# State-space stage: corrections by halves, written orders at the outputs, other slots for gating weights, two conditioning tiles held

## The chip, the cores and the metric

The kernel runs on one core of a Trainium2 chip. The metric is the device time of one execution in microseconds; smaller is better. The core's engines are TensorE (PE: matrix products, with its weight loads as PEld), VectorE (DVE), ScalarE (ACT), GpSimd (POOL) and SyncE (SP), which here only issues DMAs. Each engine has a queue of its own, and engines wait for each other by semaphores.

## What is computed

Four residual layers over 256 tokens of width 1024, all in float32, in sequence: a state-space layer with a gated feed-forward network (FFN), latent attention with an FFN, a layer with a delta-rule memory, and one with differential attention. The change touches the first of them, the state-space stage:

```
shift1, scale1, gate1, shift2, scale2, gate2 = split(silu(c) @ ada_w[0] + ada_b[0], 6)   # conditioning
h = rms_norm(x) * (1 + scale1) + shift1
s[t] = A * s[t-1] + B @ h[t]          # per group of 16 channels a complex diagonal state of 64; 64 groups
y = Re(C @ s) + D * h ;  g = gelu(y)
x = x + gate1 * (g * sigmoid(g @ w_glu + b_glu))       # gating projection
x = x + gate2 * swiglu(rms_norm(x) * (1 + scale2) + shift2)   # first FFN
```

## The kernel before

**Recurrence.** The 256 tokens are 32 chunks of 8. Inside a chunk, the output is a product of the inputs `U` with a Toeplitz kernel (`KM`, four tiles, built by `latest` and `kernels`: transposes, a split into a high and a low part, shifted products, copies by ScalarE). Between chunks the state is carried in `St` (partition = two halves of 64 states, then 32 chunks x real/imaginary x 32 groups). `into` and `turnG` bring each chunk's input into `GT`, transposed. Then VectorE takes seven serial steps, `k` = 1 to 7, over four runs of 8 chunks at once (two products and two sums a step), and then corrects the runs: for `b` = 1 to 3 the state at the end of the run before, times powers `QP`, is added to the seven chunks of run `b` (products into `w1`, sums into `St`). Four accumulators in PSUM (`psY`) hold the outputs, one for each of four blocks. They begin with the products of `U` and `KM`, and `outputs(i)` (line 1006) adds 64 products of `St` with `CE` to block `i` and copies it to `ys`. `gelu(q2)` (1021) transposes two blocks, applies gelu, and splits the result into a high part `gh` (ScalarE) and a low part `gl` (VectorE).

**Weights.** SyncE loads weights as tiles of 1 MB (`wtile`, 356) into a ring of slots: three slots of a pool that lives throughout, and after `deepen(3)` three more, in memory where tiles of the recurrence (pool `old`: `GT`, `w1` among them) lay before. The loads keep their order in the program. A gating tile holds 16 blocks of 128 x 128. `wsplit` cuts it into four pieces, each split into `whi` (ScalarE casts) and `wlo` (VectorE subtracts), and every 128 x 128 block then takes three products (`mm3`, 388). The `whi` pieces lie in slots of tag A (used by `Bm` and `St`), the `wlo` pieces in slots of tag CE (used by `CE`). `proj` (429) runs the gating projection over 64 blocks (192 products).

**Conditioning.** The vectors of the first layer come from 24 tiles of 1 MB (8 of `adaH`, 16 of `ada0`), each multiplied with the replicated activation `crep` in eight products into `ps_gv` (`gemv_rows` 581, `gemv` 595). They are generators: each call of `pump` takes one tile further, that is, issues its load and its products, and with every eighth the result is turned into a column (a ScalarE copy, four transposes, a VectorE sum). Twenty-two pumps stand ahead of the outputs; the two others stand in the gating projection, behind blocks 24 and 48 (`every` = 24).

**Order.** A planner orders the instructions of each engine by estimated times, keeping what `issue_after` and `keep_in_program_order` demand. In stretches under `manual_schedule` the named engines keep the order of the program among the instructions of that stretch; others can still be put between them. Before, TensorE and VectorE have it up to the last `turnG`, and TensorE alone in the outputs:

```
for i in range(3):
    outputs(i)
gelu(0)
outputs(3)
gelu(1)
```

## Time and profile before

| | |
|---|---|
| median of 3 runs (lowest to highest) | 1073.07 us (1072.68 to 1077.14) |
| the profiled execution, its span | 1071.87 us, 1070.1 us |
| busy: PE, PEld, DVE, ACT, POOL | 92%, 82%, 76%, 54%, 25% of the span |
| mean granted TensorE clock | 0.980 |
| read from HBM | 195.3 MB, 184 GB/s over the span |

A row of a timeline has the start (us from the span's start), the busy time, engine, line, operation, and "written<-read" by the program's names with shapes and the count of instructions merged; in square brackets the idle time of the engine before it and what ended that. Matrix products overlap, so busy times of neighbouring rows do too. `ps_gv<-raw,crep` are conditioning products, `ps_mm<-CE,St` output products, `ps_mm<-gh,whi` and the like gating products, `ps_aux<-c_cst,...` transposes. [...]

### The profile page before, as it was taken

What the parts mean: (1) busy time and instruction counts of PE and PEld (TensorE: products, weight loads), DVE (VectorE), ACT (ScalarE), POOL (GpSimd) and SP (SyncE); (2) the same over time, 40 slices, a digit from 0 to 9 for tenths busy, and PEclk for the clock granted to TensorE, in tenths of its full rate; (3) what the DMA queues carried; (4) which work ended last, traced back from release to release, by engine and by line L of the source; (5) the groups of instructions that cost most, each with busy time, mean ns of one, the idle gap of its engine ahead of it and who ended that gap; (6) DMA issues with size and microseconds to landing.
All of it is one profiled execution on the core that took longest, in us unless ns stands there. A gap on an engine that the chain in (4) does not pass through costs nothing.

```text
span 1070.1 us, 21962 instructions
## 1 busy us (share of the span) xinstructions
PE 979.8 (92%) x8474; PEld 873.8 (82%) x8474; DVE 809.3 (76%) x1771; ACT 581.7 (54%) x1304; POOL 266.4 (25%) x302
## 2 busy tenths in 40 slices
PE   3997989999999888989999999988898899899996
PEld 1655978999999866879999999987887786699974
DVE  8774799899995888769665554788887735676995
ACT  6542654555544767746555544565444344575664
POOL 6980100020012650000000011452324133243430
PEclk9999989999999999999999999999999999999998
DMA  9788549887884351256755553331312142265321
GB/s 354 286 329 332 198 158 390 337 308 299 341 335 172 119 177 40 80 197 237 264 174 193 197 176 140 130 128 52 117 41 86 55 158 76 94 231 187 125 80 39
DMA packets 29416, 198.81 MB, mean 186 GB/s; under 512 B 3744, under 2 KB 3872, under 8 KB 6528
## 3 DMA queue, kind: packets, MB, share of 16 engines
q1 hardware_dynamic: 27936, 191.73, 48.2%
q10 hardware_dynamic: 720, 3.15, 0.8%
q0 software_dynamic: 656, 2.53, 0.7%
q8 instruction: 66, 1.08, 0.4%
q14 instruction: 38, 0.31, 0.1%
HBM read 195.30 MB, written 2.10 MB: 184 GB/s over the span
## 4 chain that ended last, share of the span: by engine, by line
PE 71%; DVE 17%; ACT 4%; issue 4%; DMA 2%; POOL 2%; DVEq 0%; POOLq 0%; ACTq 0%; SPq 0%
PE ps_mm L331 52%; PE ps_aux L331 7%; PE ps_aux L334 3%; DVE wlo L310 3%; PE ps_sv L331 3%; PE ps_el L331 2%; DMA raw<-in_ada 2%; PE ps_st L331 2%; PE ps_gv L331 1%; ACT whi L380 1%; DVE Upr L310 1%; DVE D L1796 1%; POOL sq L310 1%; DVE ps_mm L310 1%; DVE shf L323 1%
## 5 line engine op out<-in xcount | busy, mean ns | idle before, releaser
L380 ACT CAST whi<-raw 128x512 fp32r<-128x512 f32 (+2 forms) x488 | 296.2, 613 | 271.3 <-PE ps_mm L331 226.0
L310 DVE TENSOR_TENSOR wlo<-raw,whi 128x512 fp32r<-128x512 f32 (+2 forms) x412 | 288.6, 714 | 127.2 <-ACT whi L380 126.6
L331 PE MATMUL ps_mm<-hh,whi 128*128 128x256 f32 x1064 | 306.8, 290 | 3.9 <-ACT hh L302 2.3
L331 PE MATMUL ps_mm<-hh,wlo 128*128 128x256 f32 x1064 | 300.5, 285 | 1.7 <-DVE wlo L310 1.7
L331 PE MATMUL ps_mm<-hl,whi 128*128 128x256 f32 x1064 | 300.3, 283 | 0.2
L331 PEld LDWEIGHTS ps_mm<-hh,whi 128*128 128x128 f32 x1064 | 202.0, 190 | 9.3 <-ACT hh L302 2.9
L331 PEld LDWEIGHTS ps_mm<-hh,wlo 128*128 128x128 f32 x1064 | 201.2, 190 | 5.9 <-DVE wlo L310 4.1
L331 PEld LDWEIGHTS ps_mm<-hl,whi 128*128 128x128 f32 x1064 | 201.9, 190 | 1.3 <-DVE hl L327 0.6
L310 POOL TENSOR_TENSOR wlo<-raw,whi 128x512 fp32r<-128x512 f32 (+2 forms) x76 | 100.1, 1317 | 241.7 <-ACT whi L380 215.9
L310 POOL TENSOR_TENSOR sq<-sq 128x256 f32<-128x256 f32 x20 | 20.4, 1018 | 406.0 <-ACT sq L302 257.6
L331 PE MATMUL ps_mm<-ah,whi 128*128 128x256 f32 x352 | 99.0, 282 | 0.0
L331 PE MATMUL ps_mm<-al,whi 128*128 128x256 f32 x352 | 98.7, 281 | 0.0
L331 PE MATMUL ps_mm<-ah,wlo 128*128 128x256 f32 x352 | 98.6, 282 | 0.0
L327 DVE SCALAR_TENSOR_TENSOR acc<-raw,cs,acc 128x512 f32<-128x512 f32 x112 | 80.0, 758 | 2.4 <-DMA raw<-in_kvada 1.3
L331 PEld LDWEIGHTS ps_mm<-ah,whi 128*128 128x128 f32 x352 | 67.2, 191 | 0.9 <-ACT whi L380 0.8
L331 PEld LDWEIGHTS ps_mm<-ah,wlo 128*128 128x128 f32 x352 | 66.3, 189 | 1.7 <-DVE wlo L310 0.8
L331 PEld LDWEIGHTS ps_mm<-al,whi 128*128 128x128 f32 x352 | 66.4, 189 | 0.0
L331 PE MATMUL ps_gv<-raw,crep 128*32 128x512 f32 x192 | 29.6, 676 | 19.1 <-DVE ps_mm L310 13.7
L331 PEld LDWEIGHTS ps_gv<-raw,crep 128*32 128x32 f32 x192 | 5.0, 114 | 24.8 <-DVE ps_mm L310 13.7
L331 PE MATMUL ps_mm<-whi,ch 128*128 128x512 f32 x48 | 19.5, 437 | 1.2 <-ACT ch L426 1.2
L331 PE MATMUL ps_mm<-oh,whi 128*128 128x256 f32 x64 | 20.1, 314 | 0.0
L331 PE MATMUL ps_mm<-whi,cl 128*128 128x512 f32 x48 | 19.8, 413 | 0.0
(558 smaller groups left out, 2030.0 us busy)
## 6 DMA issues: line engine op xcount, KB each, us to landing
raw<-in_gu SPq DMA_DIRECT2D x44, 1024.0 KB, 6.7
raw<-in_ada SPq DMA_DIRECT2D x32, 1024.0 KB, 6.2
raw<-in_dn SPq DMA_DIRECT2D x22, 1024.0 KB, 5.4
raw<-in_win SPq DMA_DIRECT2D x15, 1024.0 KB, 5.0
raw<-in_adaH SPq DMA_DIRECT2D x8, 1024.0 KB, 7.3
raw<-in_kvada SPq DMA_DIRECT2D x8, 1024.0 KB, 6.5
raw<-in_ada1h SPq DMA_DIRECT2D x8, 1024.0 KB, 5.8
raw<-in_wout SPq DMA_DIRECT2D x8, 1024.0 KB, 5.0
```

What stands on the lines that cost most here:

```text
L310: return (eng or self.nc.vector).tensor_tensor(out=out, in0=a, in1=b, op=op)
L323: (eng or self.nc.vector).tensor_scalar(out=out, in0=a, scalar1=s1, scalar2=s2, op0=op0, **kw)
L327: return self.nc.vector.scalar_tensor_tensor(out=out, in0=a, scalar=s, in1=b, op0=op0, op1=op1, **kw)
L331: return self.nc.tensor.matmul(out, l, r, start=start, stop=stop, **kw)
L334: return self.nc.tensor.transpose(out, in_, self.ident)
L380: i = self.nc.scalar.copy(out=hi[:, :width], in_=raw[:, o:o + width])
L1796: V.tensor_reduce(out=D_[64 * h:64 * h + 64, 4 * i:4 * i + 4], in_=dm[:, :, h].rearrange("p c b i -> p c i b"), axis=AX.X, op=ALU.add)
```

## The change

- Serial steps: VectorE gets a written order; the low parts of the kernel tiles (`rest`) and their products (`kernels`) stand behind steps 2, 5 and 7. A pump stands behind each step from 2 to 7, one behind the corrections' chain. The input steps pump four times, not twice; the nine pumps between kernel products are gone.
- Corrections: the chain through the run ends comes first; the products and sums then go by halves of the groups (16 of 32), in real and imaginary parts. For this the group axis of `GT`, `St` and `QP` is reordered, so that blocks 0 and 1 read the first 16 places and blocks 2 and 3 the others. `turnG` copies in four pieces, not two. The clearing of `St[:, 0]` moves to GpSimd.
- Outputs: TensorE, ScalarE and VectorE get a written order, with the splits of the first gating tile in it.
- Slots: the ring is counted from 0 at the outputs, so that the next three loads go to the three old slots. The x load stands behind the first gating load. The first `wlo` piece takes a slot of tag C (`Kmat`), the others stay with CE.
- The products of the last two conditioning tiles are held behind `self.gate`: the last gelu transpose, later the last product before their pump. The projection's work on ScalarE and VectorE is held behind the last split of `gelu(1)`.

```diff
@@ gemv
                 for g in range(n):
-                    self.mm(ps[32 * g:32 * g + 32, :], self.crep[:, k, :], ...)
+                    with self.tc.issue_after(self.gate.ins) if self.gate is not None else ExitStack():
+                        self.mm(ps[32 * g:32 * g + 32, :], self.crep[:, k, :], ...)
@@ turnG
-                    S_.copy(out=GT[:, :, ri, 8 * j2:8 * j2 + 8].rearrange("p c (j q) -> p j q c", j=2), in_=...)
+                    for jl in range(2):
+                        j = 2 * j2 + jl
+                        o = GT[:, :, ri].rearrange("p c (a j b) -> p a j b c", a=2, j=8)[:, :, j]
+                        S_.copy(out=o, in_=g[:, jl])
@@ input steps
-                if n in (1, 3):
+                if n < 4:
                     self.pump()
@@ serial steps and corrections
-            V.memset(St[:, 0], 0.0)
+            G.memset(St[:, 0], 0.0)
+            with tc.manual_schedule(engines={mybir.EngineType.DVE}):
+                rest = latest(1)
                 for k in range(1, 8):
...
+                    if k in (2, 5, 7):
+                        q = (2, 5, 7).index(k) + 1
+                        rest()
+                        kernels(q, [])
+                    if k in (3, 5):
+                        rest = latest(2 if k == 3 else 3)
+                    if k > 1:
+                        self.pump()
+                for b in range(1, 3):
...
+                self.pump()
+                runs = St.rearrange("p (b k) r g -> p b k r g", k=8)[:, 1:4]
+                for h in range(2):
+                    f = slice(16 * h, 16 * h + 16)
+                    for r in range(2):
+                        o = runs[:, :, 1:8, r, f]
+                        ws = []
+                        for e in range(2):
+                            w1 = B8("P", [128, 3, 7, 16], "w1", 4)
+                            ws.append(w1)
+                            q = QP[:, (0, 1 + r)[e], 0:7, f].unsqueeze(1).to_broadcast([128, 3, 7, 16])
+                            self.mul(w1, runs[:, :, 0:1, r ^ e, f].to_broadcast([128, 3, 7, 16]), q)
+                        for w1 in ws:
+                            self.add(o, o, w1)
-            for i in range(1, 4):
-                latest(i)()
-                kernels(i, (5, 3, 1))
@@ outputs
-            nc.sync.dma_start(out=x0, in_=a["xT"]...)
+            self.nring = 0
-            self.wparts, self.npart = [((_W(big, 4), "A"), (_W(big, 4), "CE"))], 0
+            W = lambda t: (_W(big, 4), t)
+            self.wparts, self.npart = [(W("A"), W("C"))] + [(W("A"), W("CE"))] * 3, 0
-            with tc.manual_schedule(engines={mybir.EngineType.PE}):
-                for i in range(3):
-                    outputs(i)
-                gelu(0)
-                outputs(3)
+            with tc.manual_schedule(engines={mybir.EngineType.PE, mybir.EngineType.Activation, mybir.EngineType.DVE}):
+                outputs(0, S_.copy)
+                glu(0, True)
+                outputs(1, S_.copy)
+                gelu(0, lambda: outputs(2, V.tensor_copy))      # the lambda runs behind the split of k = 1
+                for n in (8, 4, 12):
+                    glu(n, True)
+                outputs(3, S_.copy)
                 gelu(1)
+            i = nc.sync.dma_start(out=x0, in_=a["xT"]...)
+            tc.keep_in_program_order(i)
@@ gating projection
-            self.proj(glu, 0, 8, ..., 24, True, True)
+            with tc.issue_after(self.lowed.ins), tc.issue_after(self.highed.ins):
+                self.proj(glu, 0, 8, ..., 24, True, True)
```

## Rows read from the trace of the kernel before

**Rows 1.** Chain of waits, 60 to 320 us: start, us, what

```profile
88.74 14.23 DMA raw<-in_ada
...
138.61 10.27 PE ps_mm L331 x67
```

**Rows 2.** TensorE timeline, 40 to 135 us: start, us, what, idle

```profile
53.23 0.63 PE L334 MATMUL ps_aux<-c_cst,Gs 128*128 128x128 f32 x4 [0.90 <-DVE Gs L920]
...
54.69 1.04 PE L331 MATMUL ps_gv<-raw,crep 128*32 128x512 f32 x8
...
58.21 0.66 PE L334 MATMUL ps_aux<-c_cst,Gs 128*128 128x128 f32 x4 [0.42 <-DVE Gs L920]
...
86.57 5.55 PE L331 MATMUL ps_mm<-CE,St 64*32 64x128 f32 x192 [1.44 <-DVE St L310]
93.78 1.09 PE L334 MATMUL ps_aux<-c_cst,ys 128*128 128x128 f32 x8 [1.67 <-ACT ys L1018]
...
103.01 1.93 PE L331 MATMUL ps_gv<-raw,crep 128*32 128x512 f32 x8 [3.96 <-DMA raw<-in_ada]
...
106.96 1.91 PE L334 MATMUL ps_aux<-c_cst,ys 128*128 128x128 f32 x8
...
113.53 0.28 PE L331 MATMUL ps_mm<-gh,wlo 128*128 128x256 f32 x1
```

**Rows 3.** Stretches: busy time by engine, granted clock, DMA share, GB/s

```profile
68.00:70.00 2.00, 2.00 (x17) 0.97 (x15) 1.79 (x5) 0.86 (x2) 2.00 (x3) 1.00 1.01 426
84.00:86.00 2.00, 1.12 (x20) 0.21 (x8) 1.97 (x5) 0.00 (x0) 0.00 (x0) 1.00 0.13 49
102.00:104.00 2.00, 0.99 (x8) 0.20 (x8) 0.00 (x0) 0.00 (x0) 0.00 (x0) 0.50 1.02 422
170.00:180.00 10.00, 9.64 (x82) 9.44 (x81) 9.31 (x15) 5.37 (x9) 0.00 (x0) 1.00 0.99 374
```

**Rows 4.** Waits of SyncE's DMA queue, 0 to 140 us: total, times, longest

```profile
SPq L361 <- DVE St L310: 9.1, 1, 9.1
```

**Rows 5.** Timeline of ScalarE, 40 to 140 us

```profile
61.43 1.12 ACT L928 COPY GT<-ps_aux 128x256 f32<-128x256 f32 x2 [0.91 <-PE ps_aux L334]
...
91.58 1.66 ACT L380 CAST whi<-raw 128x512 fp32r<-128x512 f32 x3 [8.50 <-DMA raw<-in_wglu]
93.15 1.06 ACT L1018 COPY ys<-ps_mm 128x512 f32<-128x512 f32 x2
...
95.59 1.35 ACT L426 CAST gh<-gT 128x256 fp32r<-128x256 f32 x4
```

**Rows 6.** Timeline of VectorE, 40 to 140 us

```profile
63.41 0.42 DVE L310 TENSOR_TENSOR ps_aux<-St,ps_aux 128x256 f32<-128x256 f32 x1
...
68.09 0.17 DVE L310 TENSOR_TENSOR mods<-ps_aux,c_cols 128x16 f32<-128x16 f32 x1 [0.58 <-PE ps_aux L643]
...
77.67 0.42 DVE L310 TENSOR_TENSOR kparts<-ps_aux,kparts 128x256 fp32r<-128x256 f32 x1 [1.54 <-ACT Kmat L790]
...
90.41 0.69 DVE L1018 COPY ys<-ps_mm 128x512 f32<-128x512 f32 x1 [3.90 <-PE ps_mm L331]
...
111.73 0.75 DVE L310 TENSOR_TENSOR gl<-gT,gh 128x256 fp32r<-128x256 f32 x2
```

**Rows 7.** Timeline of TensorE, 129.5 to 139 us

```profile
130.81 0.28 PE L331 MATMUL ps_mm<-gh,wlo 128*128 128x256 f32 x1
```

**Rows 8.** Tile St, 60 to 90 us: ns min/median/max, first, last start

```profile
L310 DVE TENSOR_TENSOR St<-ps_aux,u x7: 358/424/425, 64.8 to 78.4; 128x256 f32<-128x256 f32 x6, 128x192 f32<-128x192 f32 x1
L310 DVE TENSOR_TENSOR St<-St,w x6: 611/614/626, 80.3 to 85.9; 128x448 f32<-128x448 f32 x6
L310 DVE TENSOR_TENSOR v<-St,QP x4: 215/216/225, 78.8 to 81.6; 128x64 f32<-128x64 f32 x4
```

**Rows 9.** DMA issues, 51-52 and 30-110 us: KB, us to landing

```profile
raw<-in_ada SPq DMA_DIRECT2D x1, 1024.0 KB, 5.8
...
raw<-in_wglu SPq DMA_DIRECT2D x4, 1024.0 KB, 10.5
```

More of the change, by code (lines that the diff above doesn't have):

```diff
@@ L391, in mm3 @@
         self.mm(out, wh, xl, False, False)
-        self.mm(out, wl, xh, False, last)
+        self.lastmm = self.mm(out, wl, xh, False, last)
     def stream(self, src):
@@ L424, in split @@
     def split(self, hi, lo, src, eng=None):
-        self.nc.scalar.copy(out=hi, in_=src)
+        self.highed = self.nc.scalar.copy(out=hi, in_=src)
         return self.sub(lo, src, hi.bitcast(F32), eng)
@@ L651, in s5 @@
         cp = self.cp
+        self.gate = None
         V, G, S_ = nc.vector, nc.gpsimd, nc.scalar
@@ L951, in s5 @@
                 self.table(AF.Gelu_apprx_tanh)
[L952 to L963 removed]
+            with tc.manual_schedule(engines={mybir.EngineType.DVE}):
+                rest = latest(1)
+                for k in range(1, 8):
+                    n = 4 if k < 7 else 3
+                    a8 = lambda e: A8[:, e].unsqueeze(1).to_broadcast([128, n, 2, 32])
+                    u2 = sm.tile([128, 4, 2, 32], F32, tag="u2", name="u2", bufs=2)
+                    f = slice(k, k + 8 * n - 7, 8)
+                    self.mul(u1[:, :n], St[:, f], a8(0))
+                    self.mul(u2[:, :n], St[:, f, ::-1], a8(1))
+                    self.add(u1[:, :n], u1[:, :n], GT[:, f])
+                    self.add(St[:, k + 1:k + 8 * n - 6:8], u1[:, :n], u2[:, :n])
+                    if k in (2, 5, 7):
[7 more added lines that the diff above has]
+                for b in range(1, 3):
                     v = sm.tile([128, 2, 2, 32], F32, tag="v1", name="v1", bufs=2)
@@ L1001, in s5, with outputs @@
             gl = B8("C", [128, 8, T], "gl", 4, F32R)
-            self.wparts, self.npart = [((_W(big, 4), "A"), (_W(big, 4), "CE"))], 0
+            W = lambda t: (_W(big, 4), t)
+            self.wparts, self.npart = [(W("A"), W("C"))] + [(W("A"), W("CE"))] * 3, 0
             glu = self.stream(a["wglu"])
-            def outputs(i):
+            def outputs(i, copy):
                 y = psY[i]
@@ L1017, in outputs, with gelu @@
                 o = ys[:, i // 2, :, 4 * (i % 2):4 * (i % 2) + 4].rearrange("p t j e -> p j t e")
-                (V.tensor_copy if i % 2 else S_.copy)(out=o, in_=y.rearrange("p (j t e) -> p j t e", j=4, t=8))
-            def gelu(q2):
+                copy(out=o, in_=y.rearrange("p (j t e) -> p j t e", j=4, t=8))
+            def gelu(q2, beside=None):
                 for t4 in range(2):
@@ L1029, in gelu @@
                     self.lowed = self.split(gh[:, k], gl[:, k], gT[:, k].rearrange("p t c -> p (t c)"))
-            with tc.manual_schedule(engines={mybir.EngineType.PE}):
-                for i in range(3):
-                    outputs(i)
-                gelu(0)
-                outputs(3)
+                    if beside and k == 1:
+                        beside()
+            with tc.manual_schedule(engines={mybir.EngineType.PE, mybir.EngineType.Activation, mybir.EngineType.DVE}):
[6 more added lines that the diff above has]
+                outputs(3, S_.copy)
                 gelu(1)
+            i = nc.sync.dma_start(out=x0, in_=a["xT"].rearrange("p (k t) -> p k t", k=8))
+            tc.keep_in_program_order(i)
             x1 = x0
```

35 lines of the change are left out of this document (8 added, 27 removed).

## Prediction

> **What bounds the kernel now.** I read the page first: TensorE is busy 92% of the span, so time is won where it stands still or works on something else than the next step needs. The chain of waits shows the place: from 88.74 to 102.97 us the end hangs for 14.23 us on one load of conditioning weights, and after it the chain is TensorE again [rows 1]. TensorE's own timeline tells why [rows 2]. The eight products of that conditioning tile (103.01) stand in its queue ahead of the second set of gelu transposes (106.96). The queue is served in order, so TensorE idled 3.96 us before them, and the activation those transposes feed came ten microseconds after the first half (93.78). At 102 to 104 us the granted clock is 0.50, the lower of its two levels, right behind that idle time [rows 3].
>
> Why the tile was late stands in the DMA queue. SyncE waited 9.1 us for the last state correction on VectorE [rows 4], because the next load, of gating weights, had been given a slot in memory that the corrections still used. At 84 to 86 us the queues moved 49 GB/s, against 426 GB/s at 68 to 70 [rows 3]. Six loads were then issued together; the first cast of gating weights on ScalarE waited until 91.58 [rows 5].
>
> From the low half of the last activation block (VectorE, ending 111.73 + 0.75 = 112.48) [rows 6] the rest is fixed: the 48th product of the gating projection starts at 113.53 [rows 2], the 192nd at 130.81 [rows 7], 144 in 17.28 us or 0.120 us each, and the first FFN product at 138.61 [rows 1]. So the question is how much earlier that last low half is ready, and what is added behind it.
>
> **The change, part by part.** All times below are in the profiled execution (1071.87 us, of which 1070.1 is span).
>
> *Input step, two more pumps (two more conditioning tiles).* A pump is 1.04 us of TensorE (54.69) [rows 2]. TensorE idles 0.90 us before the first transposes (53.23) and 0.42 before the third (58.21) [rows 2], where the two come to stand: 2.08 - 1.32 = 0.76 us is left, less what later steps make up. I take 0.45; the bounds are 0 and, if a tile has not landed, 2.1.
>
> *State inputs copied in the new order.* Four ScalarE copies of 128 columns take the place of two of 256, which take 1.12 us (61.43) [rows 5]. Four are between that, for as many elements, and 2.24, if each is as slow as one of 256; I take +0.2, as the copies overlap on the engine. Only the last group is on the path. The clearing of St moves to GpSimd, and a copy of the powers there gets a new order. GpSimd is full at 68 to 70 us and idle at 84 to 86 [rows 3], and only the outputs read what is cleared: nothing, or 0.8 us (84 against 83.2, below) if the clearing came last of all.
>
> *Serial steps.* They run from 63.41 [rows 6] to 78.4 + 0.36 = 78.76 [rows 8]. Two stalls stand in them: 0.58 us for a conditioning result and 1.54 for a kernel half [rows 6]. The written order puts each such subtraction behind the step by which its operands are ready, so both go: 15.35 - 2.12 = 13.23, plus the subtraction that stood before the loop (0.42): 13.65. Start 63.41 + 0.45 + 0.2 = 64.06, end 77.7. If one stall comes back (the third kernel half behind a pump), it costs its 1.5 again. Six pumps now stand inside the loop. A step is four operations 0.46 apart, 1.84 us, a tile at full rate 1.05 MB / 426 GB/s = 2.46 us [rows 3], so six tiles lose 6 x 0.62 = 3.7 us against the loop. The two earlier pumps bring the loads forward by 2 us and more (the pump at 54.69 comes to about 52.3), and of VectorE's queue only the kernel subtractions and one conditioning result could be held up: I add nothing.
>
> *Corrections by halves.* Now: two chains of four small operations (216 ns) between twelve large ones (614 ns on 448 elements) [rows 8], 78.76 to 86.53. After: the chains first, two times 0.14 + 3 x 0.25 = 0.9 us, to 79.5. Then 16 operations of 336 elements. Between 216 ns at 64 and 614 at 448, 336 is 498 ns; its bounds are 424 (256 elements) and 614. Products overlap by some 0.08, dependent sums do not, so I take 0.47 each: a half in 3.75 us (3.3 to 4.9). First half done 83.2, second 87.0.
>
> [...]
>
> But the outputs of the first two blocks read the first half alone, and that a reader waits only for the elements it reads shows in the copies out of the blocks: the second block's copy on VectorE (90.41) [rows 6] went ahead of the first block's on ScalarE (93.15) [rows 5], into interleaved columns of one tile. 192 output products take 5.55 us [rows 2], 64 take 1.85: block 0 from 83.2 to 85.1, block 1 to 87.0, and the second half of the corrections (87.0) lies beside them. That is 3.4 us off the path.
>
> *Fixed orders.* Block 1's copy on ScalarE (0.53) ends 87.6; eight transposes (1.09) [rows 2] 88.7; TensorE runs blocks 2 and 3 to 92.4 while ScalarE does two gelus and four casts (1.35) [rows 5] to 90.7. Gone: 1.67 us in which the transposes waited for block copies that stood behind casts of gating weights. Then three casts of gating weights on ScalarE, two in 1.1 us; the third needs St's memory, so it waits for block 3 (92.4) and ends 93.0. Queued behind it is block 3's copy (to 93.6), and behind that the second transposes (94.7), gelu (95.3), casts (96.7), and the last low half at 97.1 against 112.48.
>
> *Two tiles held.* Their products go behind the last transposes, into the projection: 2 x 1.05 us and one set of turning (0.6) are added to the 17.28 us. The 3.96 us of idling and the lower clock behind it go. The second tile is used at block 48 of 64, about 113; even the landing of now (102.97) would do.
>
> *Slots.* With the ring counted from 0, the first three loads (gating tile 0, gating tile 1, tile 22) go to the old slots as conditioning tiles are consumed, instead of waiting for the corrections. Tile 0 is then issued between 73 and 81 us; a load took 5.8 us with little ahead of it [rows 9], 10.5 in the burst [rows 9]: landed 79 to 91, I take 82 (the nearer row, as the queue is between full and empty there). It is wanted at 85.1. The x load moves behind it and has until 105.
>
> *Sum.* Last low half 97.1; the first 16 blocks end 1.33 us after it as now: 98.4; + 17.27 + 2.7 = 118.4, against 131.09: 12.7 us. It needs the first 24 gating products to be slipped in before the second transposes, as now; if not, 2.1 us are lost. I put half of that in: **11.5 us**, 1060.4 us in a profiled execution. The three runs shown have a median 1.2 us above the profiled one, so 1073.07 - 11.5 = **1061.5**.
>
> **Rivals.**
> *Main case, 68%*: 1058 to 1064.5.
> *Gating tile 0 still comes late, 14%.* The written order on ScalarE then turns against the kernel: its cast stands ahead of block 1's copy. For: that cast waited 8.5 us for its load [rows 5]. Against: the idle queue at 84 to 86. If it lands at 91.5 as now, copy 1 ends at 92.7 instead of 87.6: 5.1 lost, 1066.6. [...]
> *Given back in the first FFN, 11%.* If its weight stream bounds it, starting earlier gains nothing. For: DMA share 0.99 at 170 to 180 us [rows 3]. Against: TensorE is busy 9.64 of 10 there, and the loads wait for slots, which come free earlier too. Only some 2 us would stay: 1071.
> *Slower, 7%: the loop paced by loads.* TensorE's queue holds the pumps between the kernel products that VectorE's written order waits for. Rather than 1.84 us a step takes a tile's time. The two earlier pumps give a lead of two tiles, 4.9 us, which covers 2.46 a tile; the gain is gone when six tiles come (11.5 + 4.9) / 6 + 1.84 = 4.6 us apart. If each is issued only as the one before is consumed (5.8) [rows 9], six cost 6 x 3.96 = 23.8; 23.8 - 4.9 - 11.5 = 7.4 slower, 1080.5. For: one before the loop took that long. Against: three slots, and the full rate at 68 to 70 [rows 3].
>
> **How the numbers follow.** 0.5% of 1073.07 is 5.4 us, about what a measurement of this kernel tells from none; so faster is below 1067.7. Faster: 68% + nearly all of the second case (13%) = 81%. Same: the third case and the rest of the second, 12%. Slower: 7%. The range takes the first two cases whole and the edge of the third: 1057 (the sum without my allowance, one further microsecond from a quicker half) to 1070.
>
> **What would show it.** In the changed profile: no wait of TensorE for a conditioning load between 80 and 120 us; the first cast of gating weights not waiting for its load; the first output product near 83, half way through the correction operations; the last low half near 97; the granted clock 1.00 from 84 to 131; the first FFN product near 126 to 127. I am wrong if SyncE still waits for a correction before the first gating load, if TensorE stands still in the loop for loads, or if the first FFN product comes early and the span does not.

## The result, and the profile after

The change made the kernel slower: 1082.10 us (median of nine runs) against 1072.68 (nine runs of before), a ratio of 1.0092 with a 95% interval of 1.0072 to 1.0111. I had forecast 1061.5, in a range of 1057 to 1070. The ratios here and below are those over all runs, not quotients of two medians, and three slow executions, one of e6 (1093.02 us) and two of before in later comparisons, are left out of ratios and medians. The profiled execution has a span of 1079.1 us (before 1070.1), so it is 9.0 us longer. Two places of TensorE's timeline, read in both kernels, tell where. The first row of each is the transposition of the norm right ahead of the first FFN, the second a transposition 15 to 20 us from the end. First the kernel before:

```profile
136.80 0.69 PE L334 MATMUL ps_aux<-c_cst,sprd 128*128 128x128 f32 x2 [1.90 <-ACT sprd L1098]
...
1052.24 0.60 PE L334 MATMUL ps_aux<-c_cst,cp 128*128 128x128 f32 x4
```

and the changed one:

```profile
138.31 0.69 PE L334 MATMUL ps_aux<-c_cst,sprd 128*128 128x128 f32 x2 [1.89 <-ACT sprd L1129]
...
1061.28 0.60 PE L334 MATMUL ps_aux<-c_cst,cp 128*128 128x128 f32 x4
```

At the FFN the changed kernel is 1.51 us late, where I had it 11.5 early; between the two places it takes 922.97 us against 915.44, so it loses 7.53 more in stages that the diff does not touch. I call the first place "the FFN mark" and the time between the two "the later stages". There are two errors to explain, one inside the stage and one behind it.

**Inside the stage.** VectorE's timeline, which answers to [rows 6]:

```profile
63.83 0.43 DVE L310 TENSOR_TENSOR ps_aux<-St,ps_aux 128x256 f32<-128x256 f32 x1 [2.64 <-ACT St L958]
...
67.06 0.42 DVE L310 TENSOR_TENSOR St<-ps_aux,u 128x256 f32<-128x256 f32 x1
67.40 0.41 DVE L310 TENSOR_TENSOR kparts<-ps_aux,kparts 128x256 fp32r<-128x256 f32 x1
74.91 0.17 DVE L310 TENSOR_TENSOR mods<-ps_aux,c_cols 128x16 f32<-128x16 f32 x1 [7.09 <-PE ps_aux L645]
75.00 0.42 DVE L310 TENSOR_TENSOR ps_aux<-St,ps_aux 128x256 f32<-128x256 f32 x1
...
86.67 0.43 DVE L310 TENSOR_TENSOR kparts<-ps_aux,kparts 128x256 fp32r<-128x256 f32 x1 [2.57 <-ACT Kmat L795]
87.01 0.35 DVE L310 TENSOR_TENSOR v<-St,QP 128x64 f32<-128x64 f32 x2
...
88.58 0.93 DVE L310 TENSOR_TENSOR w<-St,QP 128x336 f32<-128x336 f32 x2
89.43 1.04 DVE L310 TENSOR_TENSOR St<-St,w 128x336 f32<-128x336 f32 x2
...
109.99 1.43 DVE L310 TENSOR_TENSOR gl<-gT,gh 128x256 fp32r<-128x256 f32 x4 [3.58 <-ACT gh L426]
```

The serial steps start at 63.83, and the chains at 87.01 instead of the 77.7 that I had worked out. Between the second and the third step VectorE stands still for 7.09 us, for a sum of 0.17 us: the conditioning result that one pump turns into a column. In the written order this sum stands ahead of the third step. What it waits for is on TensorE (timeline):

```profile
62.56 1.07 PE L331 MATMUL ps_gv<-raw,crep 128*32 128x512 f32 x8 [0.44 <-DMA raw<-in_ada]
...
66.28 1.94 PE L331 MATMUL ps_gv<-raw,crep 128*32 128x512 f32 x8 [2.35 <-DMA raw<-in_ada]
68.70 1.93 PE L331 MATMUL ps_gv<-raw,crep 128*32 128x512 f32 x8 [0.48 <-DMA raw<-in_ada]
70.56 2.43 PE L331 MATMUL ps_aux<-kparts,shift 128*128 128x256 f32 x11
72.92 1.07 PE L331 MATMUL ps_gv<-raw,crep 128*32 128x512 f32 x8
...
74.27 0.60 PE L645 MATMUL ps_aux<-c_cst,gemv 128*128 128x128 f32 x4
...
90.62 0.43 PE L331 MATMUL ps_mm<-CE,St 64*32 64x128 f32 x4
...
97.38 0.43 PE L331 MATMUL ps_mm<-CE,St 64*32 64x128 f32 x3 [1.45 <-issue]
98.48 1.09 PE L334 MATMUL ps_aux<-c_cst,ys 128*128 128x128 f32 x8 [0.68 <-ACT ys L1041]
99.51 5.39 PE L331 MATMUL ps_mm<-CE,St 64*32 64x128 f32 x128
...
107.80 1.04 PE L334 MATMUL ps_aux<-c_cst,ys 128*128 128x128 f32 x8
```

The four turning transposes (74.27) stand in TensorE's queue behind three more conditioning tiles and thirteen kernel products. Two of the three tiles waited for their loads, 2.35 and 0.48 us, and the granted clock fell in the first of these waits: it was 1.00 from 62 to 64 us and 0.50, the lower level, from 66 to 70, and eight products that take 1.07 us took 1.93. ScalarE had the result ready at 65.22 + 0.57. On VectorE, nothing of the third step went ahead of the waiting sum: the state that it starts from was done at 67.48 (67.06 + 0.42), and its first operation came at 75.00, behind the sum (74.91). TensorE shows the same in the kernel before: all copies into `ys` were done at 98.68 us (the last on VectorE, 98.00 + 0.68), and the second gelu transposes came at 106.96, behind products that waited for their load until 103.01.

Three of the signs that I had named for the rest of the stage came: the first output products come half way through the corrections (four at 90.62, the bulk from 92.32), no wait for a conditioning load stands between 80 and 120 us, and the first cast of gating weights no longer waits for its load, against 8.50 us before [rows 5]. ScalarE's timeline:

```profile
65.22 0.57 ACT L642 COPY gemv<-ps_gv 128x512 f32<-128x512 f32 x1
...
94.34 0.59 ACT L1041 COPY ys<-ps_mm 128x512 f32<-128x512 f32 x1 [3.25 <-PE ps_mm L331]
94.83 0.63 ACT L380 CAST whi<-raw 128x512 fp32r<-128x512 f32 x1
```

Even so, the outputs took longer than in my sum: from the end of the chains to the last low half 22.8 us (88.58 to 111.42) instead of 17.6 (79.5 to 97.1). In TensorE's rows above, it stood 1.45 us ahead of block 1's last three products (97.38; the profile shows no cause), and blocks 2 and 3 (99.51) took 5.39 us instead of 3.7, in part at the lower clock. The second transposes (107.80) then came 1.7 us after block 3's copy (done at 106.10), behind the first 24 gating products. These 24 take 2.9 us at 0.120 each, and my sum had slipped them into 1.2 us, from 92.4 to 93.6.

The last low half is done at 111.42, 14.3 us later than in my sum and 1.06 us before that of before (112.48). From there to the FFN mark it is 2.57 us longer than before, near the 2.7 that I had counted for the held tiles. The stretches [rows 3] (columns as there) show a clock of 0.83 and 0.90 where before it was 1.00 (the third row is in the middle of blocks 2 and 3):

```profile
60.00:80.00 20.00, 14.99 (x115) 5.85 (x107) 9.38 (x23) 7.60 (x21) 15.02 (x14) 0.83 0.97 371
...
80.00:100.00 20.00, 16.57 (x281) 12.48 (x285) 13.34 (x37) 6.97 (x15) 0.00 (x0) 0.90 0.63 245
...
102.00:104.00 2.00, 2.00 (x65) 1.97 (x60) 0.81 (x2) 0.73 (x2) 0.00 (x0) 0.78 1.02 426
```

SyncE's wait for a correction [rows 4] is still there, but no longer ahead of the first gating tile, which landed at 83.68:

```profile
SPq L361 <- DVE St L310: 8.6, 1, 8.6
```

**Behind the stage** TensorE's idle stretches of over 0.6 us, counted from the FFN mark on, sum to 43.3 us instead of 38.9. That is 4.4 of the 7.53 us. A part of the rest goes with the clock (granted 0.90 instead of 0.95 from 815 to 850 us, 0.95 instead of 0.98 from 850 to 960): behind the mark it stood at the lower level for 36.3 us instead of 32.2, and half of that difference, 2.1 us, is an estimate of the cost, as the lower level is half of the other (0.50 from 68 to 70 us, 1.00 from 74 to 76). The loss comes in many steps: by the same ScalarE instructions in both kernels, the change is 1.7 us late at 230 us, 2.7 at 330, 3.5 at 400, 5.3 at 550, 4.4 at 800, 5.9 at 880 and 9.0 from 960 on. Reading the program, the order of the instructions behind the stage is another one: 11 places on TensorE, 8 on VectorE and 6 on ScalarE differ from before (neighbouring differences counted as one), though neither the code nor the order of the loads there changed.

### The profile page after: what moved, and what is told of

Read it like the earlier page. It is cut to its first block, busy times and chain, and to the rows that moved or that the text cites. A ratio compares the mean times of both kernels' runs of the same rounds, so it can differ in the third digit from the quotient of the medians.

```text
span 1079.1 us, 21959 instructions
## 1 busy us (share of the span) xinstructions
PE 985.2 (91%) x8474; PEld 876.3 (81%) x8474; DVE 807.7 (75%) x1773; ACT 581.3 (54%) x1313; POOL 265.0 (25%) x303
## 3 DMA queue, kind: packets, MB, share of 16 engines
q8 instruction: 66, 1.08, 0.4%
## 4 chain that ended last, share of the span: by engine, by line
PE 68%; DVE 20%; issue 5%; ACT 4%; POOL 2%; DMA 2%; DVEq 0%; SPq 0%; POOLq 0%; ACTq 0%
PE ps_mm L331 49%; PE ps_aux L331 7%; DVE wlo L310 4%; PE ps_aux L334 3%; PE ps_sv L331 3%; PE ps_el L331 2%; PE ps_st L331 2%; PE ps_gv L331 2%; DVE acc L327 2%; ACT whi L380 1%; DVE Upr L310 1%; DMA raw<-in_ada 1%; DVE nrm L327 1%; DMA raw<-in_wkvv 1%; DVE D L1827 1%
## 5 line engine op out<-in xcount | busy, mean ns | idle before, releaser
L310 DVE TENSOR_TENSOR Upr<-NB,Us 128x16 f32<-128x16 f32 (+14 forms) x45 | 17.0, 377 | 4.5 <-ACT NB L1844 3.0
```

Source lines behind the costliest of these rows:

```text
L310: return (eng or self.nc.vector).tensor_tensor(out=out, in0=a, in1=b, op=op)
```

## The experiments

The table gives, for each kernel, the FFN mark against before (136.80) and the later stages against before (915.44), both from one profiled execution; the places in which the later order of TensorE differs from before; and the ratio over all runs. Executions differ by up to 1.5 us already at 35 us (eight transposes start at 34.32 in before and at 32.86 in e5, whose program is the same up to there), so a mark is good to that. One profiled execution is not the median either: that of e2 is the slowest of its ten (1080.93 us), that of e14 the fastest of its twelve (1065.01). So the table has a second estimate of the later loss, "by medians": the kernel's median less that of before, less the mark.

```
kernel                                     FFN mark  later   by medians  places  ratio [95%]
the change                                   +1.51  +7.53       +7.9       11   1.0092 [1.0072, 1.0111]
e1  change, ring set back                    +1.34  +3.35       +4.8        9   1.0071 [1.0040, 1.0101]
e2  before, ring reset                       -4.73  +13.80      +7.2        7   1.0029 [1.0010, 1.0047]
e3  change, VectorE free                     -7.36  +13.04     +10.1        9   1.0032 [1.0010, 1.0053]
e4  change, turning late                     -4.48  +7.00       +9.1       11   1.0044 [1.0020, 1.0067]
e5  before, ring reset and set back          -7.27  +9.44*      +2.6        0   0.9951 [0.9924, 0.9978]
e6  before, ring shifted behind the stage    -1.28  +11.39     +10.6        7   1.0085 [1.0051, 1.0118]
e7  e3, ring set back                        -7.48  +6.29       +8.4       12   1.0001 [0.9969, 1.0033]
e8  e3 without the reset                     -1.05  +8.89       +8.2       11   1.0075 [1.0052, 1.0098]
e9  e7, tiles not held                       -6.34  +6.26       +3.3        3   0.9983 [0.9961, 1.0005]
e10 e5 and corrections by halves             -1.75  +5.77       +1.6       11   0.9998 [0.9975, 1.0021]
e11 e5 and 32 small products                 +0.09  +9.68       +8.7       12   1.0078 [1.0060, 1.0096]
e12 e5 and 4 small products                  -6.41  +9.19*      -2.2        0   0.9928 [0.9903, 0.9953]
e13 e9 and 8 small products                 -10.78  +6.63       +2.9        0   0.9937 [0.9915, 0.9960]
e14 e7 and 16 small products                 -5.82  -1.06       +2.6        0   0.9975 [0.9955, 0.9995]
e15 e1 and 16 small products                 +4.66  -0.51       -0.1        0   1.0047 [1.0024, 1.0071]
* with one stall that other executions don't have, 8.6 us (see the last section)
```

### Two suspects: the written order, and the ring's counter

`wtile` takes slot `nring % len(ring)`. The reset puts the counter from 28 to 6 at the end of the stage, a shift by 2 of 6 for all later loads.

e1 puts the counter back for the later stages:

```
             self.xr = root()
             self.x = x1
+            self.nring += 22
```

> The changed kernel, with the ring's counter advanced by 22 at the end of the state-space stage, so that every later load goes to the same slot as in the kernel before. Two theories stand. T1 (stage): VectorE's written order makes the serial steps wait for a conditioning result that TensorE's queue turns late; this costs the change its gain inside the stage. T2 (slots): resetting the counter to 0 also shifts which slot every load of all later stages takes; the first gating product of FFN 2 and others are issued 15 to 36 us later, and that costs about 7.5 us between the first FFN and the end. T2 expects the stage unchanged (FFN start +1.5 us against before) and the later loss gone: about 1082 - 7.5 = 1074.5 us, ratio to before 1.000 to 1.003, the load of kva issued near 325 us again and not at 341. The rival, that the later loss comes from other differences of the planned order or from the small lag itself, expects 1080 to 1083 us (ratio 1.007 to 1.010).

Measured: 1078.86 us. The later loss falls from 7.53 to 3.35 in the profiles (from 7.9 to 4.8 by medians), but does not go. The time lies between the two forecasts, the ratio in the rival's, and its interval overlaps that of the change.

e2 is the kernel before with the reset alone (`self.nring = 0` behind `self.deepen(3)`):

> The kernel before with one line added: the ring's counter set to 0 at the gating stage; nothing else of the change. T2 (slots) expects the first gating tile issued before the corrections are done (SyncE's wait of 9.1 us gone), so that the second gelu transposes no longer wait 3.96 us, a gain of 3 to 8 us at the first FFN product (138.61 us before), and then the loss of the shifted slots in the later stages, 5 to 8 us: net ratio 0.998 to 1.004, with the load of kva near 341 us less that gain. The rival, that later losses have another cause, expects the gain to stay to the end: ratio 0.993 to 0.997.

Measured: 1075.17. The FFN mark is 4.73 early and all of it, and more, is lost later, as T2 has it: 7.2 us by medians. The 13.80 us of the profiled execution, the slowest of ten, go with the clock: behind the mark it stood at the lower level for 59.6 us instead of 32.2, and half of the difference, the same kind of estimate, is 13.7.

e3 leaves VectorE's order in the steps and corrections to the planner:

```
-            with tc.manual_schedule(engines={mybir.EngineType.DVE}):
+            with ExitStack():
```

> The changed kernel, with VectorE's order in the serial steps and corrections left to the planner instead of written by hand; pumps, halves, outputs, slots and held tiles as in the change. T1 (stage) expects the wait of 7.1 us between the second and third step gone, since the step's operations no longer stand behind the conditioning result: chains of the corrections start near 80 us instead of 87.0, the FFN 4 to 7 us earlier than with the change, 1075 to 1078 us in all (ratio 1.002 to 1.006), the later loss of 7.5 us remaining. The rival of my prediction, that the six pumps in the loop are paced by loads, expects the loop still to end past 84 us, and 1081 to 1083 us.

Measured: 1075.42. VectorE's timeline:

```profile
62.11 0.42 DVE L310 TENSOR_TENSOR ps_aux<-St,ps_aux 128x256 f32<-128x256 f32 x1
...
68.75 0.17 DVE L310 TENSOR_TENSOR mods<-ps_aux,c_cols 128x16 f32<-128x16 f32 x1 [2.09 <-PE ps_aux L645]
...
75.53 0.42 DVE L310 TENSOR_TENSOR kparts<-ps_aux,kparts 128x256 fp32r<-128x256 f32 x1 [0.98 <-ACT Kmat L795]
...
78.36 0.36 DVE L310 TENSOR_TENSOR v<-St,QP 128x64 f32<-128x64 f32 x2
```

The conditioning sum now holds the engine for 2.09 us instead of 7.09, and the chains start at 78.36 (1.5 us of that is an early start of this execution). T1 stands, and the loop is not paced by loads with all six pumps in it. The later loss is larger than expected (13.04 us, 10.1 by medians), again with long stretches at the lower clock (58.9 us).

e4 keeps the written order and puts the turning of that one result behind the corrections (the transposes and the sum go into a list that is worked off there):

```
+        def turn():
             pt = self.ps("aux")
             for j in range(4):
...
+        if self.late is None:
+            turn()
+        else:
+            self.late.append(turn)
```

> The changed kernel with VectorE's written order kept, but the turning of the one conditioning result that stands in it (four transposes of TensorE and one sum of VectorE) put behind the corrections. T1 (stage) expects the 7.1 us wait between the second and third step gone and the kernel-half wait of 2.6 us left: chains of the corrections start at 79 to 82 us instead of 87.0, the FFN 4 to 7 us earlier than with the change, 1075 to 1078 us in all (ratio 1.002 to 1.006). The rival, that the loop is paced by loads, expects only another wait in that place, for the kernel half whose products stand behind the pumps in TensorE's queue: corrections start at 84 us or later, and 1080 to 1083 us.

Measured: 1077.36. The chains start at 79.69 (87.01 with the change), and only the wait for the third kernel half is left, on VectorE:

```profile
79.35 0.42 DVE L310 TENSOR_TENSOR kparts<-ps_aux,kparts 128x256 fp32r<-128x256 f32 x1 [2.81 <-ACT Kmat L802]
79.69 0.35 DVE L310 TENSOR_TENSOR v<-St,QP 128x64 f32<-128x64 f32 x2
```

So the one sum of 0.17 us in the written order cost 6.8 us at the chains, counted from the first step (16.36 us with e4, 23.18 with the change; e4's steps start half a microsecond earlier). It was not the whole error inside the stage: e4's last low half is done at 105.43, where my sum had 97.1, and its FFN mark is 4.48 us early, not 11.5. e3 and e4 both gain 6 to 9 us at the FFN mark over the change, and both lose more behind it than they are early there.

### The slots alone

e5 is e2 with the counter set back as in e1:

> The kernel before with the ring's counter reset at the gating stage, as the change does, and advanced by 22 at the end of the state-space stage, so that the later stages take the slots that they took before. In the profile with the reset alone the first FFN started 4.7 us earlier and the end came 9 us later. T2 (the shifted slots cost the later stages) expects the gain at the FFN, 4 to 5 us, to reach the end but for what the first FFN gives back (1 to 3 us): ratio 0.996 to 0.999, and the mean granted clock back at 0.980 to 0.982. The rival T3 (an earlier start is lost later whatever the slots, above all to stretches at the lower granted clock) expects a mean clock of 0.974 to 0.978 as in the other experiments and a ratio of 1.001 to 1.005.

Measured: 1068.55, better than T2 had it; mean clock 0.983. Every instruction of TensorE, VectorE and ScalarE has the order that it has in the kernel before. The only difference is the slots of six loads, and the gain of 7 us at the FFN runs through to 410 us unchanged (7.3 us there).

e6 shifts the counter behind the stage and does nothing else (`self.nring += 2` at the end of the stage of before):

> The kernel before with the ring's counter advanced by 2 at the end of the state-space stage, and nothing else: the stage is as before, and the later stages take the slots that they take in the changed kernel. T2 (the shifted slots) expects the first FFN product where it was (138.6 us) and then a loss of 4 to 9 us by the end, ratio 1.004 to 1.008, with the load of kva issued near 340 us instead of 325.6. T3 (the slots don't matter) expects a ratio of 0.999 to 1.002.

Measured: 1082.53, a little more than T2 had, so the shift by itself costs about as much as the whole change did. SyncE's timeline shows the first load of `kva` at 342.57 instead of 325.61, TensorE's a wait of 2.99 us where before it was 1.20:

```profile
342.57 0.33 SPq L361 DMA_DIRECT2D raw<-in_kva  x1
```

```profile
223.65 1.23 PE L331 MATMUL ps_aux<-c_cst,sq 128*128 128x128 f32 x4 [2.99 <-POOL sq L310]
```

But the shift also gave TensorE another order in 7 places, so slots and order are not told apart here.

e7 is e3 with the counter set back:

> The changed kernel with VectorE's order in the steps and corrections left to the planner (first FFN product 7.4 us earlier than before in the profile) and the ring's counter advanced by 22 at the end of the stage. If T1 and T2 are the two causes and they add, the gain of the stage stays but for what the first FFN gives back (2 to 3 us): 1068 to 1070 us, ratio 0.995 to 0.998. If T3 holds (an earlier start is lost later whatever the slots), 1073 to 1076 us, ratio 1.001 to 1.004, with a mean granted clock near 0.975.

Measured: 1074.07, mean clock 0.978: the time that T3 forecast (the ratio, 1.0001, lies just below its 1.001). With both suspects gone, the stage 7.48 us early and the old slots behind it, 6.29 us are still lost (8.4 by medians). But T3 cannot be the whole of it, as e5 kept most of its gain. A third theory was needed.

### The parts of the stage

e8 is e3 without the reset:

> The changed kernel with VectorE's order left to the planner and without the reset of the ring's counter: corrections by halves, held tiles and written orders at the outputs stay, the first gating loads take the slots of before, and so do all later stages. If the reset carries the gain of the stage, gating tile 0 waits for the corrections' memory again, lands near 90 us, its cast stands ahead of the copy of block 1 on ScalarE, and the first FFN product comes 2 us early to 3 us late (136.5 to 141.5 us): ratio 0.998 to 1.004. If the halves and the written orders carry it, the first FFN product stays 5 to 8 us early and the ratio is 0.993 to 0.997.

Measured: 1079.72. It is the rival "gating tile 0 late" of the prediction, in its mechanism; at the FFN mark it cost 6.3 us (-1.05 against e3's -7.36) where I had 5.1. ScalarE's timeline and then TensorE's:

```profile
94.16 0.62 ACT L380 CAST whi<-raw 128x512 fp32r<-128x512 f32 x1 [6.58 <-DMA raw<-in_wglu]
94.68 0.58 ACT L1040 COPY ys<-ps_mm 128x512 f32<-128x512 f32 x1
```

```profile
95.32 1.97 PE L334 MATMUL ps_aux<-c_cst,ys 128*128 128x128 f32 x8 [6.62 <-ACT ys L1040]
```

The cast waits 6.58 us, block 1's copy behind it, and TensorE 6.62 us for the copy. Without the reset the written order at the outputs eats most of what the other parts bring.

e9 takes the hold off the conditioning tiles (`issue_after(self.gate.ins)` goes):

> The changed kernel with VectorE's order left to the planner, the ring's counter set back at the end of the stage, and the last conditioning tiles no longer held: their products may go as soon as they can. With them held, the projection's 24th to 96th products took about 2.6 us longer than in the kernel before. If holding is worth its price, TensorE waits 2 to 4 us for a conditioning load before the second gelu transposes, and the first FFN product comes no earlier than with them held (7.3 to 7.5 us before the kernel before); ratio 0.999 to 1.003. If not, it comes 8 to 10 us early and the ratio is 0.995 to 0.998.

Measured: 1069.51, between the two forecasts, with an interval that overlaps e7's. In one profiled execution its mark is no earlier than with the hold; e13 below, with the same stage, has it 3 us earlier than e7's. The wait of 2 to 4 us for a conditioning load did not come back (one of 0.17 us did, at 92.04).

e10 adds the corrections by halves alone to e5:

> The kernel before with the reset of the ring's counter, set back at the end of the stage (ratio 0.995 by itself), and of the change the corrections by halves alone: no further pumps, no held tiles, no written order of VectorE or ScalarE, the output blocks in TensorE's order of before. If outputs of the first two blocks start behind the first half, the first gelu transposes come 2 to 3 us earlier than without the halves (90.80 us there), but the second ones wait for the conditioning load as before: 0 to 2 us at the first FFN product, ratio 0.993 to 0.996. If the halves bring nothing, because the wait for the load takes it all, the ratio is that without them, 0.995.

Measured: 1072.35, a miss. The first gelu transposes came at 90.44, no earlier than in e5 (90.64), since TensorE's written order still has three blocks ahead of them, the third behind the second half; the wait for the conditioning load grew to 4.39 us; and 5.77 us went in the later stages (1.6 by medians).

### The later order itself

Every kernel that lost much behind the stage had another planned order there; e5, which had not, kept most of its gain. The planner goes by estimated times, so anything in the stage moves its choices for all that follows (T4). e11 and e12 change the estimates with products that compute nothing of use:

```
+            more = self.ps("aux")
+            for i in range(32):          # e12: 4
+                self.mm(more[:, 0:128], self.ident, self.ident, True, True)
             psY = [self.ps() for _ in range(4)]
```

> The kernel before with the ring's counter reset at the gating stage and set back at its end (ratio 0.995 by itself), and 32 small products of the identity with itself, into a bank that nobody reads, ahead of the first output products. TensorE has idle time there; in the profile of the kernel without them the first FFN product comes 7.3 us early, with them it comes 3 to 7 us early. They also change the costs by which the planner orders everything behind: TensorE's order differs from that of the kernel before in 13 places of the later stages, most of them in the first FFN. T4 (the planner's order of the later stages in the kernel before is a good one, and any other costs some us) expects 3 to 6 us lost between the first FFN product and the end: ratio 0.999 to 1.004. T5 (the order doesn't matter) expects what is gained at the FFN to reach the end: ratio 0.994 to 0.997.

> The same kernel with 4 of these small products instead of 32. By the program, the order of the later stages on TensorE, VectorE and ScalarE is that of the kernel before. T4 (the order of the later stages) expects the gain at the first FFN product, 6 to 7.5 us in the profile, to reach the end, but for about 1 us: ratio 0.994 to 0.997. If a shift in time alone costs the later stages, 0.998 to 1.003.

Measured: 1081.66 and 1064.26. (TensorE's order differs in 12 places behind the stage in e11; the thirteenth is the products themselves.) e11 loses more than T4 had, and e12 keeps more. The 32 products took back the gain at the FFN mark (136.89, so it is where it was before). Yet with the FFN at the old time and the old slots, 9.68 us go in the later stages; with 4 products and the old order the gain stays. So neither a shift in time nor the slots are needed for the loss; it goes with the order.

How the order makes it is not shown. By the same ScalarE instructions, e11 is 0.1 us later than before at 140 us, 2.6 at 230, 2.2 at 300, 4.1 at 420, 4.6 from 520 to 800, 8.7 at 850 and 9.8 from 940 on. But the orders differ only at 145 to 275, at 478 to 520 and at 937 to 940 us (times of before), so that more than half of the loss falls where every engine has the order of before. TensorE's stretches (busy, granted clock, DMA share, GB/s) show the largest such place, in e11

```profile
815.00:850.00 35.00, 27.85 (x316) 0.86 0.10 36
```

and in the kernel before:

```profile
815.00:850.00 35.00, 30.04 (x365) 0.95 0.09 32
```

TensorE's timeline, e11:

```profile
818.35 1.10 PE L331 MATMUL ps_el<-tw,e_w2a 128*128 128x256 f32 x4 [1.73 <-DMA e_w2a<-in_w2a]
...
844.15 1.08 PE L331 MATMUL ps_st<-R,UD 128*64 128x64 f32 x8 [2.28 <-DVE R L310]
```

before:

```profile
812.49 1.10 PE L331 MATMUL ps_el<-tw,e_w2a 128*128 128x256 f32 x4 [0.39 <-ACT X L1852]
...
838.22 0.65 PE L331 MATMUL ps_st<-R,UD 128*64 128x64 f32 x8 [1.51 <-DVE R L310]
```

The first wait is 1.34 us longer, for a load that came later. The second is 0.77 longer, and the eight products behind it take 1.08 us instead of 0.65, at a lower clock: granted 0.54 from 843 to 850 us, against 1.00 from 836 to 840 in before. It stays low for 6.8 us (0.66 from 841 to 851); before, it had fallen ahead of these products, for 3.4 (0.83 from 830 to 840). From 5.93 us at this place (844.15 - 838.22) the lag grows to 8.66 at the state products that follow. Why the load came later, and whether the other order further up brought it about, stays open.

For the last three kernels I chose the number and the place of such products so that the changed stage, ring set back, is followed by the order of before: 8 ahead of the outputs in e13 (e9's stage), 16 at the end of the stage in e14 (e7's) and e15 (e1's, the change as it is).

> The kernel without held tiles (VectorE free in the steps, ring set back; 0.9983, 6.3 us early at the FFN in its profile and 6.3 us lost behind it) with 8 small products more ahead of the outputs, by which the planner comes back to the order of the kernel before in all later stages. T4 (that order is the cause of the later loss) expects the gain at the FFN, 5 to 6.5 us, to reach the end: ratio 0.993 to 0.996, mean clock 0.981 or more. The rival (the changed stage is the cause in another way) expects 0.997 to 1.001 again.

> The changed kernel with VectorE free in the steps and the ring set back (1.0001, 7.4 us early at the FFN and 6.3 us lost behind it) with 16 small products more at the end of the stage, by which the later order is that of the kernel before. These products stand close to the path and may cost up to 2 us at the FFN. T4 expects 5 to 7 us early at the FFN and no more than 1.5 us lost behind it: ratio 0.993 to 0.997. The rival expects 0.999 to 1.003.

> The change as it is, with the ring set back at the end of the stage (1.0071, FFN 1.3 us late, 3.4 us lost behind it in the profile) and 16 small products more at the end of the stage, by which the later order is that of the kernel before. T4 expects only what the stage itself loses, 1.5 to 3.5 us with the small products: ratio 1.001 to 1.004. The rival expects 1.006 to 1.009.

Measured: 1064.27, 1068.97 and 1076.74, with ratios of 0.9937, 0.9975 and 1.0047. e13 is in T4's band; e14 and e15 lie 0.05% and 0.07% above theirs, and below the rival's, but their intervals reach into both. In e14 and e15, TensorE's two rows are

```profile
130.98 0.44 PE L334 MATMUL ps_aux<-c_cst,sprd 128*128 128x128 f32 x2 [1.90 <-ACT sprd L1133]
...
1045.36 0.60 PE L334 MATMUL ps_aux<-c_cst,cp 128*128 128x128 f32 x4
```

```profile
141.46 0.44 PE L334 MATMUL ps_aux<-c_cst,sprd 128*128 128x128 f32 x2 [1.90 <-ACT sprd L1133]
...
1056.39 0.60 PE L334 MATMUL ps_aux<-c_cst,cp 128*128 128x128 f32 x4
```

Their later stages take 914.38 and 914.93 us, 1 and 0.5 less than before, where with the planner's other order the same stages had cost 6.29 and 3.35 more. By medians the step is smaller in e14 (2.6 after 8.4 in e7) and like it in e15 (-0.1 after 4.8 in e1), and the intervals of each pair overlap. e13's profiled execution is the slowest of its six (1063.27 to 1067.71 us); it lost 6.63 later in spite of the old order, while the median keeps 8.0 of the 10.8 us. Against e9 it won nothing behind the stage (2.9 us lost by medians, after 3.3): its lead over e9 stands at the FFN mark. So an unchanged order does not make every execution alike. The clock may do a part of that: one wait is equally long in before and in e13 (2.47 us), but the four transposes behind it take 0.63 us in before, at a granted clock of 1.00 (755 to 756 us), and 1.08 in e13, where I take the clock to have fallen. TensorE's timeline, before and then e13:

```profile
755.22 0.63 PE L334 MATMUL ps_el<-c_cst,zv 128*128 128x128 f32 x4 [2.47 <-DVE e_rs L323]
```

```profile
748.50 1.08 PE L334 MATMUL ps_el<-c_cst,zv 128*128 128x128 f32 x4 [2.47 <-DVE e_rs L323]
```

Taken together: by medians the five kernels with the order of before lost -2.2 to 2.9 us behind the stage, the eleven others 1.6 to 10.6, all but e9 and e10 at least 4.8. That the order matters is shown best by e11 and e12, which differ in 28 small products and whose intervals lie far apart. How much of each loss is the order, and how much the clock of the execution, is not separated.

Two kernels, e12 and e13, beat both the change and before: 1064.3 us, 0.72% and 0.63% below before, with intervals that overlap. By e5 and e12, most of that comes from one line, the reset, if the ring is set back behind it.

## Why the prediction was wrong

**The step that failed inside the stage** is "of VectorE's queue only the kernel subtractions and one conditioning result could be held up: I add nothing". I had seen the operation and priced it at nothing; it cost 7.09 us, because its transposes queue on TensorE behind pumps that wait for loads. Without it (e4) the chains still start 2 us after my 77.7, as the wait for the third kernel half stays (2.81 us). Of the two stalls that "both go", with the order written by hand a 7.09 and a 2.57 came in their place; with it left to the planner (e3) 2.09 and 0.98. The written order helped neither. A second term was mis-sized: the outputs, from the end of the chains to the last low half, took 22.8 us instead of 17.6. The sum had no idle time and the full clock in them, and it overlapped 24 gating products with a gap of 1.2 us that holds less than half of them.

**The step that failed behind the stage** was in the sum: 118.4 against 131.09 for the projection's end, and then 1073.07 - 11.5, as if all that follows only shifted. In four of the five kernels with the order of before it did only shift (within 1.1 us in the profiled executions of e5, e12, e14 and e15, apart from the one stall; not in e13's). The change gave the later stages another order, and they took 7.53 us longer. That the order goes with such a loss is shown by e11 and e12; which waits it lengthened in the change, and how, stays open. The reset, which I counted among the gains, also outlives its stage and moves every later load by two slots; undoing that gave 2.3 us back in the change (e1, within the intervals), 3.3 in e3 and 8.4 in e2. How much of this is the slots and how much the order that they bring about stays open: I found no kernel with the shifted ring and the old order.

**The rivals.** The "slower" rival, with its 1080.5, was close in time to 1082.1, but by luck: 7.5 of the 9.4 us went behind the stage, where it had nothing. In its cause it was half right. Pumps that wait for loads do stand in TensorE's queue ahead of what VectorE waits for; but it happened once, at the conditioning result, not at each step, and without that one sum the loop ran with its six pumps (e4). "Gating tile 0 late" is real and was avoided by the reset (e8). "Given back in the first FFN" did not happen in e5, where the gain is 7.3 us at the FFN mark and 7.4 at 243 us.

**What was right.** Input steps: last transposes at 61.24, 0.50 late (0.45 taken). The 336-element operations: 0.50 us each, in 0.42 to 0.54 of the path (0.47 taken). Blocks 0 and 1 beside the second half, the early gating tile, no wait for held tiles, the last x load. The price of holding: the 24th to 96th gating products take 2.6 us longer (2.7 taken). Whether the hold is worth it is not settled: without it the FFN mark is 6.34 (e9) and 10.78 us early (e13), with it 7.48 (e7), and the intervals of e7 and e9 overlap. That e13's 10.78 is close to the 11.5 forecast is partly luck, as its last low half is 4.1 us later than my 97.1 and it doesn't pay for held tiles.

## What to carry to other kernels

In an order written by hand, ask of every operation on the list, the smallest too, which queue its operand comes through and what waits there. Where a planner orders the program by estimated times, an edit need not be local: compare the planned order of the later stages before believing that they only shift, and put counters that the edit resets back behind it. When a change moves the time by less than a per cent, judge it in a version that keeps the later order (here a handful of idle products did that), or the planner's luck is measured with it. One profiled execution can lie far from the median (5.8 us in e2): set a loss that it shows beside the medians before explaining it.

## What the runs showed of the hardware

The stall marked in the table: in e5's profiled execution, VectorE's timeline has three operations that all end at 686.69,

```profile
678.98 7.71 DVE L1818 COPY Us<-c_cst 128x128 f32<-128x128 f32 x1
679.12 7.57 DVE L310 TENSOR_TENSOR hl<-nrm,hh 128x256 fp32r<-128x256 f32 x1
679.76 6.93 DVE L1640 COPY xt<-ps_sv 128x512 f32<-128x512 f32 x1
```

while GpSimd clears tiles one after the other, the last until 686.60:

```profile
678.64 0.97 POOL L1700 MEMSET SAV<- 64x1024 f32 x1
...
685.62 0.98 POOL L1744 MEMSET BD<- 128x1024 f32 x1
```

TensorE stood still for 6.61 us. The same copy took 1.18 us in the kernel before, with the same clearing beside it, and 7.71 again in e12's profiled execution (1075.76 us), whose four quickest runs are at 1063.6 to 1064.4. So it comes in some executions only. In e5 the copy ended within 0.1 us of the last clearing (686.69 against 686.60), so it may have waited for GpSimd; no run here singles that out. No single clearing there took more than 0.98 us, and why the copy lasted through all that followed is not shown.

The clock: over the runs of each kernel its mean was 0.981 to 0.984 in e5 and e12 to e15, which keep the old order, 0.979 to 0.982 in before, 0.978 to 0.980 in e7, e9 and e10, and 0.974 to 0.976 in the change, e1 to e4, e6, e8 and e11. It differs as much between executions of one program: before went from 1068.26 us (0.988) to 1078.16 us (0.973) in the last comparison. In e11's second row a gap cost twice: 0.77 us more in itself, and 0.43 in the eight products behind it (1.08 us against 0.65), which ran at the lower level. A gap of one length, 2.47 us, was followed by transposes of 0.63 us in before and of 1.08 in e13.
